# Phase ends with a written TensorE order, and weight splits held behind the first h, in a one-core encoder step

## The chip, the cores and the metric

The kernel runs on one core of a Trainium2 chip. The metric is the device time of one execution in microseconds (us). Engines are named as in the profile: PE is TensorE's matmul, PEld its weight load, DVE VectorE, ACT ScalarE, POOL GpSimd and SP SyncE, whose queue issues nearly all DMAs here.

## The reference: what is computed

One step of a streaming encoder of two layers, width 1024, on 384 tokens: 256 of one prompt sequence and 8 x 16 of eight sample sequences. Each layer has three sub-layers (FFN, mixer, FFN). Each normalises the residual x, modulates it per sequence, and adds its gated result:

```python
def _modulate(x, g, shift, scale):
    return _rmsnorm(x, g) * (1 + scale[:, None, :]) + shift[:, None, :]

sc = jax.nn.silu(c)
for l in range(DEPTH):                       # DEPTH = 2
    mod = (sc @ prm['ada_w'][l] + prm['ada_b'][l]).reshape(c.shape[0], N_MOD, D_MODEL)   # N_MOD = 9
    x = x + 0.5 * mod[:, 2][:, None] * _swiglu(_modulate(x, g[0], mod[:, 0], mod[:, 1]), ...)
    h = _modulate(x, g[1], mod[:, 3], mod[:, 4])
    mix = ...                                # attention: two kinds in layer 0, one in layer 1
    x = x + mod[:, 5][:, None] * mix
    x = x + 0.5 * mod[:, 8][:, None] * _swiglu(_modulate(x, g[2], mod[:, 6], mod[:, 7]), ...)
y = _rmsnorm(x, prm['final_norm_g'])
```

The adaLN product `sc @ ada_w` gives 9 modulations of 1024 columns for each layer and 9 conditioning rows (one prompt, eight samples).

## The kernel before

**Layout.** The residual lies transposed, as eight tiles `xT[d]` of 128 features x 384 tokens. The input of a phase lies as `hT[0][d]` (high part) and `hT[1][d]` (rest) in the same shape: every dense product is made of three matmuls, high x high, high x rest and rest x high, so that float32 operands keep their precision.

**Weights.** `Stream` holds all dense weights as units in the order of their use. `dma()` (L179) loads a unit raw through SP; `split()` makes its two parts, a cast on ACT (L187, `wh`) and a subtraction on DVE (L188, `wl`), into three buffers, and then issues further loads, up to four raw tiles ahead. `next()` first splits until three units are there (`ahead`), so a split stands in the program well before its product; its raw tile is free for the next load once L188 is done. An FFN's first products run in `feature_half` (L501, L502 with the high part of h, then L508 with the rest): a unit is four tiles of h by 256 columns, 24 matmuls, and two units make a group.

**adaLN.** `Ada` makes one modulation at a time, in 11 steps: eight steps of four matmuls (L302), each on its own 32 columns of the array, against one 512 KB weight tile; a copy to SBUF (L307); two transposes (L311); additions on DVE (L315 and after). Each step frees its weight tile and asks for the next load (L284). Four tiles fit in general; during an FFN a pool of its own gives room for four more. `ada.step(n)` puts n steps into the program at that place, `ada.upto` sets how far steps may go.

**Phase ends.** Five times, at the ends of the first FFN, the mixer and the second FFN of layer 0, and of the first FFN and the mixer of layer 1 (ends 1 to 5 below), `close` (L483) adds the last one (FFN) or two (mixer) tiles to the residual, and makes the next phase's norm. Tiles before that have gone through `Norm.full`, which sums their squares into `acc` on POOL (L406, L408); the last ones go through `gate_p` (L474) and `gate_s` (L480, L481) on DVE and `tail` (two squares on ACT, L414; L422). `sums` (L429) sums the squares over the features with one-column matmuls, for each of three token blocks over `acc` and then the late tiles; `rstd_of` makes the root (L376) and the reciprocal (L378); `spread` scales the identity (L437, L439) and multiplies it by ones (L441), so that each token's factor stands on all partitions. `h` then makes the eight tiles: for the prompt L455 (DVE), L457 (ACT), L458 (DVE), for the samples L463 (POOL), L464 (DVE), L466 (ACT), L467 (POOL). At its end `close` puts one whole modulation (`ADA_STEPS`, 11 steps) into the program:

```python
        norm.spread(norm.sums(range(3)))
        norm.h()
        ada.upto(*norm.filled)
        ada.step(ADA_STEPS)
```

**Order.** Nothing here fixes the order on an engine. A planner orders the instructions of each engine ahead of time: it goes by costs of its own, ranks by the place in the program, and puts what is ready into holes. So adaLN steps and splits, which stand behind the norm in the program, run inside its waits where the planner sees room. On the chip each engine then takes its instructions in the planned order.

Of the kernel before, what the change touches and what calls it, by code (L numbers as in the profile page):

```python
# [17 lines left out]
D = 1024  # L18
KD = 8
# [19 lines left out]
class Weave:  # L39
    """Work in stages, advanced in turn between the dense products."""  # L40
# [46 lines left out]
    def over(self, slots):  # L87
        """A callback that spreads what is queued over so many calls."""
        count = iter(range(slots, 0, -1))
        return lambda: self.pace(next(count, 1))  # L90
# [14 lines left out]
def kernel(  # L105
# [43 lines left out]
    # ------------------------------------------------------------ constants  # L149
# [13 lines left out]
    # ------------------------------------------------------------ weights  # L163
    class Stream:
        """Weights in the order of their use: loaded in units, split exactly into two parts of 12 bits each."""

        def __init__(self):
            self.units = []
            self.nd = self.ns = self.nu = 0
            self.depth = 2  # L170
            self.tiles, self.parts = [], {}

# [10 lines left out]
        def split(self):  # L183
# [3 lines left out]
            act.copy(out=h, in_=src)  # L187
            dve.tensor_tensor(out=lo, in0=src, in1=h.bitcast(F32), op=ALU.subtract)  # L188
# [9 lines left out]
        def next(self, held=0):  # L198
            """The next unit; the last held ones are still in use."""
# [40 lines left out]
    def add_out(w, parts):  # L240
        """parts: the pairs of rows that a pass over all columns takes."""
# [26 lines left out]
    # ------------------------------------------------------------ adaLN: one modulation of 1024 columns at a time  # L268
# [3 lines left out]
    class Ada:  # L272
# [15 lines left out]
        def ahead(self):  # L288
            """Loads as far as there is room; what a phase's own pool holds is used within the phase."""
# [31 lines left out]
        def finish(self, l, m, d, n):  # L321
            """A factor of a norm becomes 1 + itself, times the gain; a gate of an FFN is halved."""
# [8 lines left out]
        def half_load(self, pl, m, half):  # L331
            """Half of the columns of a modulation of the first norm."""
# [29 lines left out]
        def upto(self, l, m):  # L362
            """Steps past this modulation are put off."""
# [9 lines left out]
    # ------------------------------------------------------------ norms  # L373
# [7 lines left out]
    def warm(x):  # L381
        """The table of the square root, in time."""
# [8 lines left out]
    class Norm:  # L391
        """The norm of the residual and its modulation: full() as tiles become final, tail() for the last ones."""
# [30 lines left out]

        def sums(self, blocks):
# [7 lines left out]
        def spread(self, rs):  # L432
            """The factors of the tokens, over the partitions."""
# [11 lines left out]
        def h(self, ds=range(KD)):  # L445
            for d in ds:
                new_h(d)
                self.h_prompt(d, self.bc)
                self.h_sample(d, self.bs)

        def h_prompt(self, d, bc):
# [5 lines left out]
            act.activation(out=h, in_=u, func=AF.Identity, bias=sh, scale=1.0)  # L457
            dve.scalar_tensor_tensor(out=lo, in0=u, scalar=sh, in1=h.bitcast(F32), op0=ALU.add, op1=ALU.subtract)  # L458
# [24 lines left out]
    def close(l, mod, ds, ys, norm):  # L483
        """The last tiles of the residual, and the norm; a modulation of a later product fills the wait."""
# [4 lines left out]
        norm.spread(norm.sums(range(3)))  # L489
        norm.h()  # L490
        ada.upto(*norm.filled)
        ada.step(ADA_STEPS)

    # ------------------------------------------------------------ FFN
# [99 lines left out]
    def out_half(l, ks, d0, mod, slot, done=None, left=None):  # L594
        """Four of the tiles, over pairs of rows ks, gated and added to the residual."""
# [33 lines left out]
    def token_chunk(n, weave, slots):  # L629
        """Token-major product over n columns: banks of prompt blocks 0 and 1, and of the sample tokens."""  # L630
# [13 lines left out]
    def token_cols(slot):  # L644
        """Token-major product over 256 columns: a bank for each block of tokens."""
# [22 lines left out]
    def soft_rows(S, regions, scale, P, n_rows=128):  # L668
        """Unnormalised exponentials of the rows of S over each region into P; the reciprocals of their sums."""
# [917 lines left out]
```

## Time and profile before

| | us |
|---|---|
| median of 3 runs | 1668.05 |
| lowest, highest | 1667.81, 1672.78 |
| span of the profiled execution, first to last instruction | 1666.9 |
| TensorE busy in it | 1637.8 |
| VectorE busy, ScalarE busy, GpSimd busy | 781.7, 648.9, 125.5 |

The times do not say which run the profiled one is closest to; beside the span no other time of the profiled execution is given. Its mean granted TensorE clock is 0.996 of full speed. In the rows, a matmul of float32 operands on 32 columns appears as two records, and so does a one-column sum; a timeline merges neighbours of one kind (x20 means 20 records), gives the start, the time from the first one's start to the last one's end, and in brackets the idle time before it with what ended it. Matmuls overlap, so the next one starts before the row's end.

### The profile page before, as it was taken

To read this page: it belongs to the slowest core of one execution; us is meant where nothing else is said; L and a number is where in the kernel's file an instruction comes from. 1 tells how busy PE (TensorE), PEld (TensorE's weight loads), DVE (VectorE), ACT (ScalarE), POOL (GpSimd) and SP (SyncE) were. 2 spreads that over 40 slices of the span, in tenths; PEclk is the share of its full clock that TensorE was granted. 3 is DMA by queue.
4 is the path that set the end of the run, shared out by engine and by line. 5 is a ranking of instruction groups with operands and counts; after the bars stand their busy time and mean duration, and the time that the engine had idled before them with its cause. 6 is when DMAs were issued, how large, how long until landed. Compare 5 with 4: busy or idle time off the path is not lost.

```text
span 1666.9 us, 27050 instructions
## 1 busy us (share of the span) xinstructions
PE 1637.8 (98%) x10877; PEld 1496.5 (90%) x10877; DVE 781.7 (47%) x1500; ACT 648.9 (39%) x1205; POOL 125.5 (8%) x186
## 2 busy tenths in 40 slices
PE   7999999999999999999999999999999999999998
PEld 5999999977777799999989999998888879999998
DVE  4543334444466843344453433436554675343334
ACT  4433322353445533333243333324555554333334
POOL 2000001110000300000120000002000012000021
PEclk9999999999999999999999999999999999999999
DMA  9855555482464765663465555345777664444344
GB/s 333 291 157 161 176 158 167 134 275 67 140 209 135 251 165 147 182 192 116 130 210 175 154 165 170 120 122 164 254 230 238 190 207 138 127 127 127 120 123 143
DMA packets 235136, 287.14 MB, mean 172 GB/s; under 512 B 11834, under 2 KB 205154, under 8 KB 235011
## 3 DMA queue, kind: packets, MB, share of 16 engines
q1 hardware_dynamic: 234754, 285.24, 54.9%
q8 instruction: 86, 1.41, 0.4%
q14 instruction: 40, 0.32, 0.1%
q0 software_dynamic: 112, 0.10, 0.0%
q10 hardware_dynamic: 144, 0.07, 0.0%
HBM read 268.10 MB, written 17.27 MB: 171 GB/s over the span
## 4 chain that ended last, share of the span: by engine, by line
PE 94%; DVE 2%; issue 1%; DMA 1%; ACT 1%; POOL 0%; POOLq 0%; ACTq 0%; DVEq 0%
PE bank L501 16%; PE bank L508 15%; PE bank L502 15%; PE bank L264 12%; PE bank L265 11%; PE bank L266 11%; PE bank L302 4%; PE bank L663 2%; PE bank L1224 1%; PE bank L1292 1%; PE bank L839 0%; DMA ada<-in_ada_w_dram 0%; PE bank L344 0%; PE bank L1273 0%; PE bank L973 0%
## 5 line engine op out<-in xcount | busy, mean ns | idle before, releaser
L188 DVE TENSOR_TENSOR wl<-raw,wh 128x1024 fp32r<-128x1024 f32 (+1 forms) x338 | 402.3, 1192 | 612.5 <-ACT wh L187 611.6
L187 ACT CAST wh<-raw 128x1024 fp32r<-128x1024 f32 (+1 forms) x338 | 345.1, 1022 | 611.2 <-PE bank L508 243.7
L501 PE MATMUL bank<-h,wh 128*128 128x384 f32 x1472 | 499.2, 341 | 3.8 <-ACT h L466 3.8
L502 PE MATMUL bank<-h,wl 128*128 128x384 f32 x1472 | 492.2, 336 | 0.0
L501 PEld LDWEIGHTS bank<-h,wh 128*128 128x128 f32 x1472 | 276.2, 188 | 26.0 <-issue 10.4
L508 PE MATMUL bank<-h,wh 128*128 128x384 f32 x1472 | 287.8, 335 | 0.0
L502 PEld LDWEIGHTS bank<-h,wl 128*128 128x128 f32 x1472 | 276.4, 188 | 3.2 <-issue 1.8
L508 PEld LDWEIGHTS bank<-h,wh 128*128 128x128 f32 x1472 | 257.8, 188 | 0.6 <-issue 0.5
L264 PE MATMUL bank<-ah,wh 128*128 128x384 f32 (+1 forms) x704 | 235.1, 334 | 0.0
L266 PE MATMUL bank<-al,wh 128*128 128x384 f32 (+1 forms) x704 | 233.5, 332 | 0.0
L265 PE MATMUL bank<-ah,wl 128*128 128x384 f32 (+1 forms) x704 | 233.5, 332 | 0.0
L264 PEld LDWEIGHTS bank<-ah,wh 128*128 128x128 f32 x704 | 132.3, 188 | 3.3 <-issue 2.9
L265 PEld LDWEIGHTS bank<-ah,wl 128*128 128x128 f32 x704 | 132.3, 188 | 0.0
L266 PEld LDWEIGHTS bank<-al,wh 128*128 128x128 f32 x704 | 132.3, 188 | 0.0
L264 PE MATMUL bank<-wh,h 128*128 128x256 f32 (+3 forms) x312 | 103.8, 335 | 0.1
L266 PE MATMUL bank<-wl,h 128*128 128x256 f32 (+3 forms) x312 | 98.7, 317 | 0.0
L265 PE MATMUL bank<-wh,h 128*128 128x256 f32 (+3 forms) x312 | 98.4, 316 | 0.2 <-POOL h L467 0.2
L532 ACT ACTIVATE s<-bank 128x384 f32<-128x384 f32 x88 | 38.5, 489 | 130.7 <-PE bank L508 130.7
L302 PE MATMUL bank<-ada,scT 128*32 128x256 f32 x1024 | 83.3, 390 | 2.9 <-DMA ada<-in_ada_w_dram 2.3
L538 DVE TENSOR_TENSOR a<-s,bank 128x384 f32<-128x384 f32 x88 | 44.9, 551 | 78.7 <-PE bank L508 78.7
L264 PEld LDWEIGHTS bank<-wh,h 128*128 128x128 f32 x312 | 59.0, 190 | 12.3 <-issue 9.7
L265 PEld LDWEIGHTS bank<-wh,h 128*128 128x128 f32 x312 | 59.2, 190 | 3.5 <-issue 0.8
(311 smaller groups left out, 1543.7 us busy)
## 6 DMA issues: line engine op xcount, KB each, us to landing
raw<-in_ffn_w_in_dram SPq DMA_DIRECT2D x176, 512.0 KB, 3.8
ada<-in_ada_w_dram SPq DMA_DIRECT2D x128, 512.0 KB, 4.6
raw<-in_ffn_w_out_dram SPq DMA_DIRECT2D x68, 512.0 KB, 3.5
raw<-in_ffn_w_out_dram SPq DMA_DIRECT2D x34, 384.0 KB, 3.1
raw<-in_c_w_in_dram SPq DMA_DIRECT2D x24, 512.0 KB, 4.8
half<-in_ada_w_dram SPq DMA_DIRECT2D x16, 512.0 KB, 10.0
out_dram<-kv SPq DMA_DIRECT2D x32, 224.0 KB, 5.2
raw<-in_ab_w_in_dram SPq DMA_DIRECT2D x12, 512.0 KB, 5.5
```

The costliest lines, as they stand in the source:

```text
L187: act.copy(out=h, in_=src)
L188: dve.tensor_tensor(out=lo, in0=src, in1=h.bitcast(F32), op=ALU.subtract)
L264: pe.matmul(out=out, lhsT=wh, rhs=xh, start=start, stop=False)
L265: pe.matmul(out=out, lhsT=wl, rhs=xh, start=False, stop=False)
L266: pe.matmul(out=out, lhsT=wh, rhs=xl, start=False, stop=stop)
L302: pe.matmul(out=ps[32 * g:32 * g + 32, 0:256], lhsT=scT[:, k, :], rhs=t[:, g * 256:(g + 1) * 256], start=(k == 0), stop=(k == KD - 1), til ...
L501: pe.matmul(out=out, lhsT=w[0][:, kk, ms], rhs=hT[0][k], start=(k == 0), stop=False)
L502: pe.matmul(out=out, lhsT=w[1][:, kk, ms], rhs=hT[0][k], start=False, stop=False)
L508: pe.matmul(out=banks[mi][:, 0:NT], lhsT=w[0][:, kk, mi * 128:(mi + 1) * 128], rhs=hT[1][k], start=False, stop=(k == KD - 1))
L532: act.activation(out=s[mi], in_=g[mi][:, 0:NT], func=AF.Silu)
L538: dve.tensor_tensor(out=a, in0=s[mi], in1=u[mi][:, 0:NT], op=ALU.mult)
L663: pe.transpose(out=ps[0:m, i * 128:(i + 1) * 128], in_=src, identity=ident)
```

## The change

`close` now writes TensorE's order out, in a region in which TensorE issues its instructions in the order of the program: the sums of `acc` for three blocks, three adaLN steps, the sums of the late tiles, three adaLN steps, the spread, two adaLN steps. What else falls in between on TensorE, and the other engines, stay the planner's. The three last steps of the modulation come behind h. All sums of a norm now go into one accumulation (`sum_part`), of which the first matmul alone starts anew. `h` returns its prompt instructions, and the next two splits after a phase end are ordered behind those of tiles 1 and 3: the cast behind that tile's L457 on ACT, the subtraction behind its L458 on DVE, as an order on the engine and not a wait. Nothing else is changed; the diff also drops docstrings and comments, which make no instruction.

```diff
+    def behind(later, first):
+
+        tc.add_manual_dep(later.ins if hasattr(later, "ins") else later, (first.ins if hasattr(first, "ins") else first).name,
+                          mybir.DependencyInfo(mybir.DependencyClass.NoSync, mybir.DependencyReason.DATA), reason="order")
...
             self.tiles, self.parts = [], {}
+            self.after = []
...
-            act.copy(out=h, in_=src)
-            dve.tensor_tensor(out=lo, in0=src, in1=h.bitcast(F32), op=ALU.subtract)
+            cast = act.copy(out=h, in_=src)
+            sub = dve.tensor_tensor(out=lo, in0=src, in1=h.bitcast(F32), op=ALU.subtract)
+            if self.after:
+                for later, first in zip((cast, sub), self.after.pop(0)):
+                    behind(later, first)
...
+        def sum_part(self, ps, sq, blocks, first=False):
+
+            for i, b in enumerate(blocks):
+                pe.matmul(out=ps[:, i:i + 1], lhsT=sq[:, b * 128:(b + 1) * 128], rhs=ones[:, 0:1], start=first and i == 0, stop=True, skip_group_check=True)
...
         def h(self, ds=range(KD)):
+            made = []
             for d in ds:
                 new_h(d)
-                self.h_prompt(d, self.bc)
+                made.append(self.h_prompt(d, self.bc))
                 self.h_sample(d, self.bs)
+            return made
...
-        norm.spread(norm.sums(range(3)))
-        norm.h()
         ada.upto(*norm.filled)
-        ada.step(ADA_STEPS)
+        with tc.manual_schedule(engines={mybir.EngineType.PE}):
+            ps = bank()
+            norm.sum_part(ps, norm.acc, range(3), True)
+            ada.step(3)
+            for sq in norm.late:
+                norm.sum_part(ps, sq, range(3))
+            ada.step(3)
+            norm.spread(rstd_of(ps[:, 0:3], 3, D))
+            ada.step(2)
+        made = norm.h()
+        stream.after = [made[1], made[3]]
+        ada.step(ADA_STEPS - KD)
```

## Rows read from the trace of the kernel before

**Rows 1.** From the page: the span, the first engine of its part 1 (busy us, share of the span, instructions), and the chain that ended last by engine.

```profile
span 1666.9 us, 27050 instructions
PE 1637.8 (98%) x10877; PEld 1496.5 (90%) x10877; DVE 781.7 (47%) x1500; ACT 648.9 (39%) x1205; POOL 125.5 (8%) x186
PE 94%; DVE 2%; issue 1%; DMA 1%; ACT 1%; POOL 0%; POOLq 0%; ACTq 0%; DVEq 0%
```

**Rows 2.** Busy time of each engine in the stretches from a phase's last product to the next phase's first, at ends 3 and 4; then the granted clock and DMA.

```profile
852.27:860.01 7.74, 7.10 (x81) 3.68 (x80) 4.67 (x12) 3.51 (x10) 1.69 (x4) 1.00 0.84 253
1149.84:1159.84 10.00, 8.44 (x99) 4.33 (x98) 7.11 (x16) 4.19 (x10) 2.77 (x6) 1.00 0.87 272
```

**Rows 3.** Timeline of TensorE at end 3, from the first sum to the spread.

```profile
852.11 0.28 PE L429 MATMUL bank<-ones,acc 128*128 128x1 f32 x2
852.32 1.49 PE L302 MATMUL bank<-ada,scT 128*32 128x256 f32 x20
...
853.98 0.36 PE L429 MATMUL bank<-ones,acc 128*128 128x1 f32 x2
...
854.43 0.36 PE L429 MATMUL bank<-ones,acc 128*128 128x1 f32 x2
854.72 0.63 PE L302 MATMUL bank<-ada,scT 128*32 128x256 f32 x6
855.28 0.38 PE L429 MATMUL bank<-ones,sq 128*128 128x1 f32 x2
855.60 1.50 PE L302 MATMUL bank<-ada,scT 128*32 128x256 f32 x24
857.03 0.91 PE L441 MATMUL bank<-dg,ones 128*128 128x384 f32 x2
```

**Rows 4.** The same of end 5: the third adaLN piece, and the spread.

```profile
1374.23 0.62 PE L302 MATMUL bank<-ada,scT 128*32 128x256 f32 x2 [0.28 <-DMA ada<-in_ada_w_dram]
1375.13 0.88 PE L441 MATMUL bank<-dg,ones 128*128 128x384 f32 x2 [0.28 <-DVE dg L439]
```

**Rows 5.** Timeline of VectorE among the gates: end 1, end 4, end 5.

```profile
326.00 0.83 DVE L188 TENSOR_TENSOR wl<-raw,wh 128x640 fp32r<-128x640 f32 x1
...
1152.62 0.23 DVE L481 TENSOR_TENSOR xT<-gt,xT 128x128 f32<-128x128 f32 x1
...
1370.11 1.22 DVE L188 TENSOR_TENSOR wl<-raw,wh 128x1024 fp32r<-128x1024 f32 x1
1371.24 0.29 DVE L481 TENSOR_TENSOR xT<-gt,xT 128x128 f32<-128x128 f32 x1
```

**Rows 6.** VectorE while h is made: two L458 one tile apart, behind end 3 (timeline), and all L464 of the kernel (least, median and greatest ns).

```profile
861.13 0.47 DVE L458 SCALAR_TENSOR_TENSOR h<-up,modT,h 128x256 fp32r<-128x256 f32 x1
...
862.39 0.47 DVE L458 SCALAR_TENSOR_TENSOR h<-up,modT,h 128x256 fp32r<-128x256 f32 x1
...
L464 DVE TENSOR_TENSOR us<-us,modT x48: 273/544/551, 23.2 to 1385.9; 128x128 f32<-128x128 f32 x48
```

**Rows 7.** Timeline of TensorE at end 1 (first sum, spread) and end 4 (spread); windows that cut a merged row show it alone.

```profile
325.04 0.28 PE L429 MATMUL bank<-ones,acc 128*128 128x1 f32 x2
...
330.37 0.59 PE L441 MATMUL bank<-dg,ones 128*128 128x384 f32 x1
...
1156.30 0.59 PE L441 MATMUL bank<-dg,ones 128*128 128x384 f32 x1
```

**Rows 8.** Four adaLN loads ahead of end 5: the first in the chain that ended last (start, us), the four issues on SP's queue (ns, first and last start), and the issue to landing of the last.

```profile
1358.24 3.85 DMA ada<-in_ada_w_dram
...
L284 SPq DMA_DIRECT2D ada<-in_ada_w_dram x4: 341/376/384, 1358.2 to 1359.6; - x4
...
DMA to landing us min/median/max: 6.1/6.1/6.1
```

**Rows 9.** Timelines behind end 2, where the last tiles of h are made: VectorE, GpSimd, ScalarE, TensorE.

```profile
575.72 1.22 DVE L188 TENSOR_TENSOR wl<-raw,wh 128x1024 fp32r<-128x1024 f32 x1
576.85 1.28 DVE L458 SCALAR_TENSOR_TENSOR h<-up,modT,h 128x256 fp32r<-128x256 f32 x2
...
575.95 1.30 POOL L467 TENSOR_TENSOR h<-us,h 128x128 fp32r<-128x128 f32 x1 [0.90 <-ACT h L466]
...
576.19 0.28 ACT L466 CAST h<-us 128x128 fp32r<-128x128 f32 x1
...
577.42 1.55 PE L508 MATMUL bank<-h,wh 128*128 128x384 f32 x8
```

**Rows 10.** Timeline of TensorE in the second FFN: the last adaLN records of the modulation begun at end 2, and the product behind one of the pieces.

```profile
602.82 0.62 PE L302 MATMUL bank<-ada,scT 128*32 128x256 f32 x2
...
628.21 0.63 PE L302 MATMUL bank<-ada,scT 128*32 128x256 f32 x6
628.77 0.45 PE L501 MATMUL bank<-h,wh 128*128 128x384 f32 x1
...
633.51 0.64 PE L302 MATMUL bank<-ada,scT 128*32 128x256 f32 x8
```

**Rows 11.** adaLN matmuls (L302) alone, in five stretches from the last product of a phase to the end of the next phase's first group (at end 1: of its first four units): us, PE busy (records), PEld busy, clock, DMA; the first, the last and the sum of the five, whose records are 90, 48, 66, 82 and 64.

```profile
325.20:346.70 21.50, 6.81 (x90) 2.75 (x90) 1.00 0.91 302
...
1369.47:1388.95 19.48, 5.51 (x64) 1.90 (x64) 1.00 0.49 175
sum 100.97, PE 27.99 PEld 10.80; mean PE 5.60 PEld 2.16
```

More of the change, by code (lines that the diff above doesn't have):

```diff
@@ L456, in h_prompt @@
             h, lo = hT[0][d][:, PR], hT[1][d][:, PR]
-            act.activation(out=h, in_=u, func=AF.Identity, bias=sh, scale=1.0)
-            dve.scalar_tensor_tensor(out=lo, in0=u, scalar=sh, in1=h.bitcast(F32), op0=ALU.add, op1=ALU.subtract)
+            return (act.activation(out=h, in_=u, func=AF.Identity, bias=sh, scale=1.0),
+                    dve.scalar_tensor_tensor(out=lo, in0=u, scalar=sh, in1=h.bitcast(F32), op0=ALU.add, op1=ALU.subtract))
         def h_sample(self, d, bs):
```

## The prediction, made blind

> **What bounds the kernel now.** I read the page first. TensorE is busy for 98% of the span and holds 94% of the chain that ended last [rows 1], so two things can move the time: work that TensorE does, and moments in which it has none. The change touches five places, the ends of the phases, so next I read the stretches from the last product of a phase to the first product of the next. The shortest is end 3 with 7.74 us, the longest end 4 with 10.00, both at granted clock 1.00, the upper of the two levels [rows 2]; no term below comes from the clock. TensorE looks busy there, but mostly with adaLN steps that fill the wait for a chain: gates (DVE), squares (ACT), sums (PE), root (ACT), reciprocal and diagonal (DVE), spread (PE), h (DVE, ACT, POOL).
>
> The timeline of TensorE at end 3 [rows 3] shows the order that the planner chose: one sum, adaLN, sums, adaLN, the last sum, adaLN, spread. The 64 records of a modulation are 8 steps of four matmuls side by side, two records each. A piece of 20 records takes 1.49 us and one of 6 takes 0.63, so a pass of four costs (1.49 - 0.63) / 2 = 0.43 and a piece 0.20 on top; a cut pass costs a whole one: at end 5 a piece of 2 records takes 0.62 [rows 4]. The timeline of VectorE at ends 5 and 1 [rows 5] has a weight split (L188: 1.22 us, or 0.83 for the narrower units at end 1) in the middle of the gates, just ahead of L481, for whose result the square of the sample tokens waits.
>
> After the spread VectorE is full: the three operations on a tile of h come round every 1.26 us (861.13 to 862.39 [rows 6]), and in an FFN a tile's products take TensorE only 4 x 0.17 = 0.70 (8 matmuls take 1.55, the last one's tail included [rows 9]). So for the first 10 us of a phase VectorE sets the pace, not TensorE.
>
> **The change, part by part.**
>
> *Order of sums, adaLN and spread.* Nothing is added: the same sums, 8 steps and spread. At end 3, from [rows 3]: three sums of the accumulator from 852.11 at a pitch of 0.225 (853.98 to 854.43 for two) reach 852.79; three steps start at 852.85 and let TensorE go 1.43 later (855.60 to 857.03), at 854.28; the last of three late sums starts at 854.73 instead of 855.28. Three more steps follow 0.32 behind it and the spread comes at 856.48 instead of 857.03: 0.55 us earlier. The split in the gates matters less than it looks, since the late sums now stand behind three steps anyway. The same 4.37 us behind the first sum puts the spread of end 1 at 329.41 instead of 330.37 [rows 7]: 0.96 earlier. At end 4 L481 starts as late as 1152.62, behind a memset [rows 5]. If that keeps its place, the squares end near 1153.2, the last sum starts at 1153.65 and the spread at 1155.40 instead of 1156.30 [rows 7]: 0.90 earlier, and some 1.3 more if the memset moves away; I keep the smaller gain.
>
> Ends 2 and 5 close the mixers, which hold only four adaLN buffers, so tiles 5 to 8 are loaded while the steps run. End 5 already waits for the DMA of tile 5 at 1374.23, and the spread is let past after one matmul of it [rows 4]. The new order must finish tiles 5 and 6 first. One sum more stands ahead of step 1 (0.225), whose end frees the buffer, so tile 5 lands at about 1374.45. Of four such loads the first, issued at 1358.24, landed after 3.85 us and the last, issued at 1359.6, after 6.1 [rows 8]: 1.23 apart. That puts tile 6 at 1375.7, its pass behind it, and the spread at 1376.1 instead of 1375.13: 1.0 later. Bounds: 0.3 later if tile 6 lands only one pass (0.43) behind tile 5; 0.8 earlier if neither is late, as at end 3; I take the measured spacing. End 2 has the same buffers and sums, and I give it the same 1.0. Over the five chains: -0.96 + 1.0 - 0.55 - 0.90 + 1.0 = -0.41 us.
>
> *Splits behind h.* No split is added, and one that stands in the gap costs little, because VectorE is waiting there. Behind the second and fourth h it stands where VectorE has no free time. At an FFN's end one of the two held splits comes from the gap (the other waits for its buffer until the phase is under way, and stands there today); at a mixer's end both do. That is one of 0.83 at end 1 and 2 + 1 + 1 + 2 of 1.22 at ends 2 to 5: 0.83 + 6 x 1.22 = 8.15 us of VectorE put ahead of later h. Queued behind a held subtraction are the next tiles' L455, L458 and L464, for which ACT, POOL and then the products wait; behind the held cast stands the next h on ACT. Lower bound nothing, if planner and hardware find holes; upper bound 8.15. Today's split inside the stretch at end 2 [rows 9] is nearly free, because its subtraction (575.72) delays only the last two L458, whose products come last; one behind tile 1 or 3 is ahead of everything, so I take 8.15, less what TensorE has in hand: the last h is there at 576.47 and the last part of the second half starts at 577.42, 0.95 later where the tile's products need 0.70. So 0.25 at each of ends 2 to 5: -1.0.
>
> Could POOL catch up during a subtraction, so that the next L464 takes its least, 0.27, instead of its median of 0.54 [rows 6]? That would give back 0.27 for each of seven splits, 1.9 in all. The row says no: a POOL L467 that ran beside the split at 575.72 took 1.30 us, until 577.25, past the split's end at 576.94 [rows 9]. The Trainium skill, page "SBUF — State Buffer", section "Who interferes with whom", says that a VectorE instruction with two SBUF inputs and a GpSimd instruction that reads SBUF exclude each other; by it the sum stays, without it the sum would be 1.9 lower.
>
> A held split also releases its raw buffer later, so the weight load that waits for it moves some 7 us back on SP's queue. It serves a unit several units (of 24 matmuls, 4.2 us each) ahead, and no longer stands ahead of adaLN loads; I cost it at nothing, and at one wait of 1 to 2 us if a unit does come late.
>
> *What goes into the longer waits.* At end 2 the last 16 of the 64 records stand today among the dense products, in pieces of 2, 6 and 8 [rows 10]; from the start of one to the next product is 0.56 us (628.21 to 628.77). In the new order they run before the first product: -1.7. At ends 1, 3 and 4 the planner already pulls later steps into the stretch (end 1 has 90 records of adaLN in it, 26 more than a modulation [rows 11]); as VectorE holds TensorE up for longer, I count one step more at each, 3 x 0.56 = -1.7, with the bounds 0 and -1.7.
>
> **Sum.** -0.41 + 8.15 - 1.0 - 1.7 - 1.7 = +3.3 us. The profiled execution's span of 1666.9 becomes 1670.2; the median of the runs lies 1.15 above that span, so the time is 1668.05 + 3.3 = 1671.4, 0.2% slower: inside the 0.3% (5 us) that I take as the least that a measurement tells from no change.
>
> **Rivals.**
> - *A, slower: the held subtractions fall behind the last h.* The planner ranks h first, and VectorE has no hole. An FFN's first group needs its second unit some 6 us after its first product; a subtraction later than that decides it. At end 2 the last L458 would end at 578.13 - 1.22 + 1.0 = 577.91 and the subtraction at 579.13; 23 matmuls at 0.174 and the last one's tail then end at 583.3 instead of 578.97 [rows 9], +4.3, less the 1.7; at end 5 the same +4.3; end 1 even; ends 3 and 4 keep their 0.55 and 0.90. +5.5: 1673.5. For it: the ranks. Against: today's subtraction at 575.72 got in ahead of two L458.
> - *B, slower: nothing of the stretch is hidden.* Neither the 1.0 nor the second 1.7 come: +6.0, 1674.1. For it: POOL is blocked along with VectorE. Against: the steps pulled in today.
> - *C, faster: only TensorE's own work counts.* If every wait is filled with adaLN that is needed anyway, as 98% busy suggests, what matters is that no pass is cut. From the ends to the end of the first group, adaLN takes 27.99 us for 90 to 64 records in each stretch, 350 in all [rows 11]. Uncut, 350 / 8 passes at 0.43 are 18.8, and three pieces at each end 15 x 0.20 = 3.0: 21.8. -6.2: 1661.9. Against: at end 5 there is no later modulation to fill with, and VectorE sets the pace behind each spread.
> - *No effect* lies within the forecast: at end 3 the fixed order is nearly the old one.
>
> **Chances.** Forecast 0.41, A 0.16, B 0.14, C 0.29. So faster by over 0.3% 0.29, within 0.41, slower 0.30. The range goes from 1661, just under C, to 1676, which is B with a late weight unit (2 us); the forecast's own goes from 1667 (no effect, or holes for half of the splits) to 1673.
>
> **What would show it.** Right: spreads 4.4 us behind the first sum at ends 1 and 3, and about 1 us later than now at ends 2 and 5, with a wait for DMA in the second three steps; L188 close behind the second and fourth L458; a last L458 that stands 1.2 us (2.4 at ends 2 and 5) further from the spread. A shows as TensorE waiting for wl in the first group; C as first groups that end no later than now, with adaLN pieces of 24, 24 and 16 records. The prediction is wrong if spreads don't wait for tile 6, if splits find holes that these rows don't show, or if the planner, set off by the new order, rearranges adaLN among the dense products, at 0.56 us for each piece.

## The result, and the profile after

The changed kernel takes 1685.94 us (median; 1684.51 to 1687.74) against 1667.93 us for the kernel before on the same chip: ratio 1.0102, 95% interval 1.0087 to 1.0116. It is 18 us slower, far outside the forecast range. The page of the kernel after: span, TensorE, and the chain that ended last, by engine.

```profile
span 1684.8 us, 27051 instructions
PE 1643.0 (98%) x10877; PEld 1497.5 (89%) x10877; DVE 781.3 (46%) x1500; ACT 646.8 (38%) x1205; POOL 118.9 (7%) x186
PE 92%; DVE 3%; issue 2%; ACT 1%; DMA 1%; POOL 0%; POOLq 0%; ACTq 0%; DVEq 0%
```

Beside [rows 1] the instructions of TensorE are the same 10877, but they are busy 5.2 us longer, and TensorE stands idle in the other 12.7 us of the 17.9 by which the span grew. The same number of instructions at a longer duration is a first hint of a lower clock, no more.

Where the time went is seen best by phase. Each end begins with TensorE's first sum, so the starts of these sums cut the span into six phases. The table holds the length of each phase in the profiled execution, less the same phase of the kernel before (325.04, 234.19, 292.88, 297.57, 219.63 and 297.58 us); the experiments of the next section are in it too.

```
                 to end 1  end 1-2  end 2-3  end 3-4  end 4-5  from end 5
after              +0.01    -0.15   +11.83    +0.29    +1.10    +4.83
no_hold            +0.60    -1.63   +12.44    -1.00    +0.30    +0.59
hold_only          +0.12    -1.82    +3.37    +0.24    -0.58    +3.73
early_spread       +0.15    -3.18    +8.44    -1.01    +0.33    -0.65
held_ranked        +0.46    -1.88   +12.58    -0.31    +0.23    +2.38
end2_only          +0.40    -1.81   +12.52    -0.01    +1.34    +0.70
mod_first          +0.42    -2.53    +5.85    -1.00    +0.31    -0.30
ffn_order          -0.24    -2.37    +0.51    -1.01    +0.30    +1.31
ffn_then_free      -0.45    +0.24    +1.32    -1.02    +0.35    +1.00
three_ends         +0.57    -4.40    +0.73    -0.98    -0.16    -0.81
four_ends          -0.33    -2.72    -0.02    -1.00    +0.31    -1.03
```

The phases between ends 1 and 2 and between ends 4 and 5 are the mixers. Between ends 1 and 2 the last four runs and mod_first have the same order written and the same adaLN records in the mixer, and range from -4.40 to +0.24; between ends 4 and 5 runs that leave end 4 as it was range from -0.58 to +1.34. So single microseconds of these two columns mean nothing. The phase that begins at end 2 holds two thirds of the loss, the phase that begins at end 5 another quarter.

End 3 went as forecast. TensorE there, to be read beside [rows 3]:

```profile
863.80 0.72 PE L436 MATMUL bank<-ones,acc 128*128 128x1 f32 x6
864.45 1.50 PE L311 MATMUL bank<-ada,scT 128*32 128x256 f32 x24
865.88 0.83 PE L436 MATMUL bank<-ones,sq 128*128 128x1 f32 x6
866.64 1.50 PE L311 MATMUL bank<-ada,scT 128*32 128x256 f32 x24
868.08 0.91 PE L455 MATMUL bank<-dg,ones 128*128 128x384 f32 x2
```

Two uncut pieces of 24 records, no wait, and the spread 4.28 us behind the first sum instead of 4.92. End 2 has the same program and looks otherwise (TensorE again, from the first sum to the first product):

```profile
559.09 0.83 PE L436 MATMUL bank<-ones,acc 128*128 128x1 f32 x6 [0.45 <-POOL acc L417]
559.85 1.50 PE L311 MATMUL bank<-ada,scT 128*32 128x256 f32 x24
561.28 1.50 PE L436 MATMUL bank<-ones,sq 128*128 128x1 f32 x12
562.71 0.64 PE L311 MATMUL bank<-ada,scT 128*32 128x256 f32 x8
564.80 0.64 PE L311 MATMUL bank<-ada,scT 128*32 128x256 f32 x8 [1.46 <-DMA ada<-in_ada_w_dram]
567.54 1.08 PE L311 MATMUL bank<-ada,scT 128*32 128x256 f32 x8 [2.10 <-DMA ada<-in_ada_w_dram]
568.55 1.65 PE L455 MATMUL bank<-dg,ones 128*128 128x384 f32 x2
...
571.98 0.69 PE L526 MATMUL bank<-h,wh 128*128 128x384 f32 x1 [0.76 <-ACT h L482]
```

The second three steps wait 1.46 us for adaLN tile 5 and 2.10 for tile 6, and the spread, which needs neither, comes 9.46 us behind the first sum, where it came 5.92 before. The last 8 records take 1.08 us instead of 0.64, and the spread's two matmuls 1.65 instead of 0.9. The windows behind show why (us, TensorE busy, PEld, DVE, ACT, POOL, then granted clock, DMA share and GB/s):

```profile
562.00:566.00 4.00, 1.99 (x23) 1.01 (x23) 0.66 (x3) 0.66 (x2) 0.00 (x0) 1.00 0.84 287
566.00:570.00 4.00, 2.46 (x10) 0.70 (x10) 0.00 (x0) 0.00 (x0) 0.00 (x0) 0.58 0.99 356
570.00:574.00 4.00, 3.24 (x20) 1.23 (x19) 3.42 (x8) 3.05 (x7) 3.06 (x7) 0.50 0.71 233
574.00:578.00 4.00, 4.00 (x19) 3.73 (x16) 4.00 (x12) 3.30 (x9) 3.10 (x7) 0.64 0.50 154
578.00:582.00 4.00, 4.00 (x34) 2.98 (x33) 4.00 (x10) 3.07 (x8) 1.48 (x3) 1.00 0.09 12
```

Behind the wait TensorE was granted its lower level (0.50 is 1.2 of 2.4 GHz) until about 577, while the first products already ran; the kernel before holds 1.00 throughout this place. The DMA share is 0.99 in the window in which TensorE waits. The change did not add that load: the kernel before has shares of 0.95 and 1.04 in its windows from 562 to 566 and from 566 to 570, at a clock of 1.00. What is new is that the spread now stands behind the whole of tiles 5 and 6.

The rest of that phase's loss lies in the FFN that follows. First the whole stretch from the spread of end 2 to the first sum of end 3, of the kernel before and of the kernel after:

```profile
565.15:852.11 286.96, 285.83 (x1684) 277.88 (x1685) 122.99 (x170) 99.12 (x140) 17.64 (x23) 1.00 0.53 158
```

```profile
568.55:863.80 295.25, 292.84 (x1741) 281.24 (x1737) 125.29 (x175) 100.66 (x143) 15.72 (x23) 0.99 0.55 164
```

It is 8.29 us longer with 57 more TensorE records. The adaLN matmuls alone (same columns as [rows 11]), in the mixer ahead of end 2 and in the FFN behind it, before and after:

```profile
344.00:559.00 215.00, 13.87 (x168) 4.72 (x168) 0.98 0.53 169
565.30:852.00 286.70, 8.05 (x94) 2.93 (x94) 1.00 0.53 158
```

```profile
344.00:559.00 215.00, 8.94 (x110) 2.20 (x110) 0.98 0.48 149
568.70:863.50 294.80, 12.15 (x144) 4.30 (x144) 0.99 0.55 164
```

Before, the planner had done 168 records in the mixer; after, 110. The missing 58 did not make the mixer shorter to speak of (-0.15 in the table), but 50 of them came back in the FFN, where TensorE has hardly any gaps, and cost 4.10 us of busy time. Counted from first sum to first sum, the kernel before has 256 adaLN records between ends 1 and 2 and 128 between ends 2 and 3, the changed kernel 192 and 192: one whole modulation of 64 records has moved.

At end 5 the spread comes 6.88 us behind the first sum instead of 5.82. The larger loss comes behind it, in the first group (TensorE, then VectorE):

```profile
1397.71 0.86 PE L526 MATMUL bank<-h,wh 128*128 128x384 f32 x4
1401.48 0.62 PE L527 MATMUL bank<-h,wl 128*128 128x384 f32 x2 [2.91 <-DVE wl L194]
```

```profile
1398.09 1.31 DVE L474 SCALAR_TENSOR_TENSOR h<-up,modT,h 128x256 fp32r<-128x256 f32 x2
1399.33 0.86 DVE L471 SCALAR_TENSOR_TENSOR up<-bank,modT,xT 128x256 f32<-128x256 f32 x2
1400.22 1.21 DVE L194 TENSOR_TENSOR wl<-raw,wh 128x1024 fp32r<-128x1024 f32 x1
1401.35 0.87 DVE L474 SCALAR_TENSOR_TENSOR h<-up,modT,h 128x256 fp32r<-128x256 f32 x2
1402.25 2.35 DVE L194 TENSOR_TENSOR wl<-raw,wh 128x1024 fp32r<-128x1024 f32 x2
```

The held subtraction (L194) is not right behind the second or fourth tile of h; it stands among the last ones, at 1400.22, and TensorE waits 2.91 us for it. In the window from 1402 to 1406, right behind, the granted clock is 0.61. At end 2 TensorE has no such wait for a subtraction.

### The profile page after: what moved, and what is told of

The parts are those of the page before. It is cut to its first block, busy times and chain, and to the rows that moved or that the text cites. A ratio compares the mean times of both kernels' runs of the same rounds, so it can differ in the third digit from the quotient of the medians.

```text
span 1684.8 us, 27051 instructions
## 1 busy us (share of the span) xinstructions
PE 1643.0 (98%) x10877; PEld 1497.5 (89%) x10877; DVE 781.3 (46%) x1500; ACT 646.8 (38%) x1205; POOL 118.9 (7%) x186
## 4 chain that ended last, share of the span: by engine, by line
PE 92%; DVE 3%; issue 2%; ACT 1%; DMA 1%; POOL 0%; POOLq 0%; ACTq 0%; DVEq 0%
PE bank L526 16%; PE bank L527 15%; PE bank L533 15%; PE bank L273 11%; PE bank L275 11%; PE bank L274 11%; PE bank L311 3%; PE bank L688 2%; PE bank L1249 1%; PE bank L1317 1%; DVE us L480 0%; PE bank L864 0%; PE bank L353 0%; PE bank L998 0%; DVE h L474 0%
## 5 line engine op out<-in xcount | busy, mean ns | idle before, releaser
L194 DVE TENSOR_TENSOR wl<-raw,wh 128x1024 fp32r<-128x1024 f32 (+1 forms) x338 | 402.3, 1192 | 609.1 <-ACT wh L193 608.2
L526 PEld LDWEIGHTS bank<-h,wh 128*128 128x128 f32 x1472 | 277.4, 189 | 29.4 <-issue 10.6
```

The costliest lines, as they stand in the source:

```text
L194: sub = dve.tensor_tensor(out=lo, in0=src, in1=h.bitcast(F32), op=ALU.subtract)
L526: pe.matmul(out=out, lhsT=w[0][:, kk, ms], rhs=hT[0][k], start=(k == 0), stop=False)
```

## The experiments

All are compared with the kernel before on the same chip. Unless a diff says otherwise it stands against the changed kernel.

**Without the holds** (no_hold), to split the loss between the two halves of the change:

```diff
-        stream.after = [made[1], made[3]]
```

> The changed kernel with the splits not held behind h; TensorE's order at the ends stays written out. Theory 1 (held subtractions fall behind the last h, and TensorE waits for them at ends 2 and 5): the 2 to 3 us waits for wl in the first groups go, and most of what ends 2 and 5 lost behind the spread with them; what stays is the late spread of ends 2 and 5 and the adaLN that moved into the dense products. 7 to 10 us over the kernel before. Rival (the written order alone costs the 18 us, through its waits for DMA and the lower clock behind them; splits are nearly free): 15 us or more over the kernel before.

Measured: 1679.47 us against 1668.83, ratio 1.0072 (1.0047 to 1.0097), +10.6 us. That is a little above the 7 to 10 of the first theory and far below the rival. By the medians the holds cost some 7 us of the 18; by the table 4.24 of them lie behind end 5. The phase of end 2 is no shorter without them (+12.44), so its loss is the order's.

**The holds alone** (hold_only; against the kernel before, whose close is kept):

```diff
-        norm.h()
+        made = norm.h()
+        stream.after = [made[1], made[3]]
```

> The splits held behind h, TensorE's order at the ends left to the planner as before. Theory 1: the waits for wl at ends 2 and 5 are there (about 3 us each), spreads are where they were or a little earlier, adaLN lies as before: 5 to 9 us over the kernel before. Rival (the written order does it all): within 2 us of the kernel before.

Measured: 1673.48 against 1668.83, ratio 1.0028 (1.0018 to 1.0037), +4.7, just under the 5 to 9 expected. TensorE's waits in this run, from the list of them (total us, times, longest):

```profile
PE bank L519 <- DVE wl L194: 4.0, 2, 2.0
```

Two waits for a held subtraction, one behind each mixer; the kernel before has none. The loss behind end 5 is +3.73, so the hold does there by itself what it does in the changed kernel. Alone the holds cost 4.7 us, on top of the written order some 7; the intervals are too wide to tell the two apart.

**The spread ahead of the tiles that are late** (early_spread; no holds). At the mixers' ends the late sums are followed by one step, and four come behind the spread:

```diff
-            ada.step(3)
+            ada.step(3 if len(ds) == 1 else 1)
             norm.spread(rstd_of(ps[:, 0:3], 3, D))
-            ada.step(2)
+            ada.step(2 if len(ds) == 1 else 4)
         made = norm.h()
-        stream.after = [made[1], made[3]]
```

> Splits not held; written order, but at the two mixers' ends only one adaLN step (tile 4, which is loaded) stands between the late sums and the spread, and four behind it. Theory 1: the spread of end 2 comes at about 564 and that of end 5 about 1.5 us earlier than in the run with the full order and no hold, TensorE's clock stays at its upper level there, and the time is 3 to 5 us below that run, so 3 to 6 over the kernel before; the rest is adaLN among the dense products of layer 0's second FFN. Rival (the wait for tiles 5 and 6 only moves behind the spread, where the products wait for it): within 1 us of that run.

Measured: 1674.40 against 1668.83, ratio 1.0045 (1.0028 to 1.0061), +5.6, 5 us below no_hold. TensorE at end 2:

```profile
559.82 0.64 PE L311 MATMUL bank<-ada,scT 128*32 128x256 f32 x8
561.06 0.88 PE L455 MATMUL bank<-dg,ones 128*128 128x384 f32 x2 [0.60 <-DVE dg L453]
561.87 0.64 PE L311 MATMUL bank<-ada,scT 128*32 128x256 f32 x8
564.38 0.64 PE L311 MATMUL bank<-ada,scT 128*32 128x256 f32 x8 [1.86 <-DMA ada<-in_ada_w_dram]
```

The spread is 4.86 us behind the first sum, the adaLN tile is waited for behind it (1.86 us), while h is made, and the clock stays at 1.00. Still the phase of end 2 loses 8.44 us: the late spread and the clock are not the whole.

**The holds with a place that is enforced** (held_ranked). The splits are issued in the program between tiles of h, so that nothing lets them fall behind:

```diff
-        made = norm.h()
-        stream.after = [made[1], made[3]]
+        stream.after = [norm.h(range(2))[1]]
+        stream.split()
+        stream.after = [norm.h(range(2, 4))[1]]
+        if len(ds) == 2:
+            stream.split()
+        norm.h(range(4, KD))
```

> The changed kernel, but the held splits stand in the program between the tiles of h, so that the planner ranks them ahead of later h: subtractions stand right behind h of tiles 1 to 3 instead of behind the last one. The prediction's price: each pushes the rest of h back by up to 1.22 us, no wait for wl. Theory 1: waits for wl of 3 us at ends 2 and 5 are exchanged for up to 2.4 us of later h: 0 to 4 us below the changed kernel. Rival (a subtraction finds holes on VectorE once it is ranked): the last L474 stands no further from the spread than in the kernel before, and the time falls by 6 us or more.

Measured: 1683.78 against 1668.83, ratio 1.0094 (1.0076 to 1.0112). VectorE behind end 5, the subtractions now among the tiles:

```profile
1391.77 1.48 DVE L194 TENSOR_TENSOR wl<-raw,wh 128x1024 fp32r<-128x1024 f32 x1
1393.17 0.68 DVE L474 SCALAR_TENSOR_TENSOR h<-up,modT,h 128x256 fp32r<-128x256 f32 x1
...
1394.17 0.28 DVE L480 TENSOR_TENSOR us<-us,modT 128x128 f32<-128x128 f32 x1
...
1396.29 1.21 DVE L194 TENSOR_TENSOR wl<-raw,wh 128x1024 fp32r<-128x1024 f32 x1
```

In no_hold one subtraction, too, stands ahead of the last L474 of end 5 (at 1399.31):

```profile
1398.08 1.32 DVE L194 TENSOR_TENSOR wl<-raw,wh 128x1024 fp32r<-128x1024 f32 x1
```

This is the kernel that I had priced. From the spread to the end of the last L474 it takes 14.49 and 14.48 us at ends 3 and 4, against 13.12 and 13.27 in no_hold: 1.4 and 1.2. At end 5 it is 14.07 - 13.11 = 0.96. At each of these ends held_ranked has two subtractions ahead of the last L474 and no_hold has one, so each of these figures is the price of one more, of 1.22. Behind a subtraction the next L480 can take its least, 0.28 at 1394.17; four of the eight at end 5 do, against one in no_hold. TensorE no longer waits for wl behind end 5, and that phase loses 2.38 instead of 4.83. In all it is 15.0 us above the kernel before, 3 less than the changed kernel, since end 2 keeps its loss (+12.58).

**The order at end 2 alone** (end2_only; the other four ends and the splits as in the kernel before):

```diff
+        if l == 0 and len(ds) == 2:
+            ada.upto(*norm.filled)
+            with tc.manual_schedule(engines={mybir.EngineType.PE}):
...
+        else:
+            norm.spread(norm.sums(range(3)))
...
```

> The kernel before with the written order (3, 3 and 2 adaLN steps, as in the changed kernel) at end 2 alone; no split is held, the other four ends are as before. Theory (end 2 is where the order loses: 3.4 us by the wait for its adaLN tile 6, some 2 us by the clock behind that wait, 4 to 6 us by the modulation that it pins out of the mixer): 8 to 12 us above the kernel before, with a lag that rises by 4 us or more between the spread of end 2 and 592 us and by 4 us or more between 592 and 718 us. Rival (only the late spread counts, and the rest came from the other ends or the holds): 2 to 5 us above.

Measured: 1681.59 against 1667.51, ratio 1.0075 (1.0059 to 1.0091), and +12.52 us in the phase of end 2, as in the changed kernel. Its two parts, up to the spread and from there to end 3:

```profile
557.82:566.66 8.84, 5.91 (x66) 3.35 (x66) 4.31 (x11) 2.78 (x7) 0.00 (x0) 0.88 0.67 229
566.66:863.22 296.56, 294.73 (x1749) 280.42 (x1746) 123.46 (x173) 99.56 (x141) 17.51 (x23) 0.99 0.56 166
```

2.92 us of it are the late spread, 9.60 the FFN behind. In all it is 14.1 us, more than the 8 to 12 that I expected. On the same products of the FFN the lag behind the kernel before rises by 4.2 us from the spread to 592 and by 5.6 from there to 718, both the 4 or more of the theory. So one end out of five makes the larger part of the loss, and the rival (2 to 5 us) is out.

**The modulation asked for ahead of the gates** (mod_first; against early_spread), so that it is not inside the written stretch of end 2:

```diff
+        if l == 0 and len(ds) == 2:
+            ada.upto(*norm.filled)
+            ada.step(ADA_STEPS)
+            ada.upto(1, 1)
+        else:
+            ada.upto(*norm.filled)
         for d, y in zip(ds, ys):
             gate_p(l, mod, d, y)
             gate_s(l, mod, d, y)
             norm.tail(d)
-        ada.upto(*norm.filled)
```

> The run with the early spread and no holds, with one difference: at end 2 the modulation that was due there, the third of the second norm's FFN, is asked for ahead of the gates and outside the fixed stretch, so that the planner may again do it in the idle stretches of the mixer; the fixed stretch at end 2 takes eight steps of the next modulation, as the gap did in the kernel before. Theory (the fixed stretch pins that modulation behind the mixer, and 48 to 64 records more then stand between the dense products of the FFN behind end 2): the 6 us that the early-spread run lost in that FFN go away, and the run is at the kernel before or up to 3 us below it. Rival (the loss in that FFN has another cause, for example the clock or the order of the loads): 4 to 6 us above the kernel before, as the early-spread run.

Measured: 1671.37 against 1667.51, ratio 1.0020 (1.0008 to 1.0033): +3.9, just short of the rival's 4 to 6. But the rows say more than the sum. adaLN alone, in the mixer and in the FFN as above, then that FFN as a whole, then the same whole of early_spread:

```profile
344.00:557.00 213.00, 13.45 (x168) 4.47 (x168) 0.99 0.52 170
562.10:855.50 293.40, 7.65 (x96) 1.89 (x96) 0.99 0.53 155
...
561.99:855.85 293.86, 288.33 (x1687) 278.16 (x1688) 122.18 (x170) 99.02 (x140) 17.63 (x23) 0.99 0.53 155
```

```profile
561.06:857.52 296.46, 292.96 (x1753) 280.35 (x1754) 123.71 (x173) 99.22 (x141) 17.74 (x23) 0.99 0.57 169
```

The records moved as the theory says: 168 in the mixer and 96 in the FFN, where the kernel before has 168 and 94, and TensorE's busy time in the FFN falls by 4.63 us. But the stretch is only 2.60 shorter, since TensorE now idles 293.86 - 288.33 = 5.53 us in it where it idled 3.50. Two places make the idle time; the first one (ScalarE, then TensorE):

```profile
682.19 0.87 ACT L561 ACTIVATE s<-bank 128x384 f32<-128x384 f32 x2 [6.81 <-PE bank L537]
682.95 2.94 ACT L193 CAST wh<-raw 128x1024 fp32r<-128x1024 f32 x3
```

```profile
684.05 0.62 PE L530 MATMUL bank<-h,wh 128*128 128x384 f32 x2 [1.77 <-ACT wh L193]
685.31 0.62 PE L531 MATMUL bank<-h,wl 128*128 128x384 f32 x2 [0.64 <-DVE wl L194]
```

Three casts stand in one lump behind an activation (L561) that needs the group's last product, so TensorE waits for the cast and then for its subtraction, 2.4 us, and the same again 20 us later; in the window from 700 to 710 the granted clock is 0.83. So the pinned modulation is one cause, shown and priced at 4 to 5 us of busy time, of which this run gets 2.60 us of time back. It is not the whole: the FFN of mod_first still takes 6.90 us more than that of the kernel before (293.86 against 286.96), 4.40 of them idle. Late casts are a second cause in this run; the changed kernel and early_spread have one such place each in that FFN, with waits of 0.5 us for the cast and 0.6 for the subtraction, and the kernel before, ffn_order and end2_only have none. What in the planner's inputs puts the casts there was not tried and stays open.

**The order at the FFN ends alone** (ffn_order), and **with the sums alone fixed at the mixers' ends** (ffn_then_free, no adaLN in those stretches); no holds in either:

In ffn_order the ends with one tile (`len(ds) == 1`) keep the written order and the others are closed as before; in ffn_then_free these others have

```diff
+            with tc.manual_schedule(engines={mybir.EngineType.PE}):
+                ps = bank()
+                norm.sum_part(ps, norm.acc, range(3), True)
+                for sq in norm.late:
+                    norm.sum_part(ps, sq, range(3))
+                norm.spread(rstd_of(ps[:, 0:3], 3, D))
+            norm.h()
+            ada.upto(*norm.filled)
+            ada.step(ADA_STEPS)
```

> The written order of sums, adaLN, late sums, adaLN and spread stands at the three ends behind an FFN only (ends 1, 3 and 4); the two ends behind a mixer (2 and 5) are closed as in the kernel before, and no split is held. Theory (the order is a small gain wherever its adaLN tiles have landed and no modulation is moved out of the mixers): the run without holds and with an early spread was 0.66 us ahead across end 1, 0.9 across end 3 and 0.4 behind across end 4, so this run should be 0 to 3 us below the kernel before. Rival (the order costs something at the FFN ends too, by the adaLN that stands one step further ahead or by the extra DMA): 2 us or more above the kernel before.

> The written order at the FFN ends, and at the two mixer ends a fixed order of the sums, the late sums and the spread alone, with no adaLN in it; no split is held. Theory (what hurts at the mixer ends is the adaLN in the fixed stretch, not the order of the sums): the modulation moves back into the mixer, TensorE does not wait for an adaLN tile ahead of the spread, and the run is 0 to 4 us below the kernel before. Rival (sums that are no longer interleaved with adaLN as the planner had them cost as well at these ends): 2 us or more above the run that fixes the FFN ends alone.

Measured: ffn_order 1667.15 against 1667.51, ratio 0.9995 (0.9985 to 1.0004); ffn_then_free 1668.64, ratio 1.0009 (0.9999 to 1.0018). The order at the FFN ends costs nothing, and the rival is out. In all seven runs that write end 3 without holds the phase from there is 0.98 to 1.02 us shorter. At end 4 the spread comes 5.31 us behind the first sum instead of 6.62, and yet the phase from there is 0.30 to 0.35 longer in the six runs that write it without holds: no gain is seen. ffn_then_free shows that a fixed order without adaLN in it does not pin the modulation (the phase of end 2 loses 1.32 instead of 12), but it delays the spread at ends 2 and 5 to 6.78 and 6.74 us; it is 1.5 us above ffn_order, which neither theory had.

**What is left worth having** (three_ends and four_ends): ends 1, 3 and 5 written, end 5 with 3, 1 and 4 steps; four_ends writes end 4 as well. Ends that are not named are closed as before; no holds.

```diff
+        if l == 1 and len(ds) == 2:
...
+                ada.step(1)
+                norm.spread(rstd_of(ps[:, 0:3], 3, D))
+                ada.step(4)
...
+        elif len(ds) == 1 and l == 0:
...
+                ada.step(3)
+                norm.spread(rstd_of(ps[:, 0:3], 3, D))
+                ada.step(2)
...
+        else:
+            norm.spread(norm.sums(range(3)))
...
```

In four_ends the second condition is `len(ds) == 1` alone.

> The written order only where a run showed a gain: ends 1 and 3 with 3, 3 and 2 adaLN steps, end 5 with 3 steps ahead of the late sums, one behind them and four behind the spread; ends 2 and 4 are closed as in the kernel before, and no split is held. Theory (the gains of the single ends add: 0.7 to 1 us at each of ends 1 and 3, 0.8 at end 5, and the 0.4 that end 4 lost is not lost): 2 to 4 us below the kernel before, and 1 to 3 us below the run that fixes the three FFN ends. Rival (these gains are of the size by which the planner's orders of the stretches between differ, and do not add up): within 1.5 us of the kernel before.

> As the run with ends 1, 3 and 5 written, and end 4 written too (3, 3 and 2 steps); end 2 is closed as in the kernel before. Theory (at end 4 the 0.9 us by which the chain is shorter is given back, since the planner had put 32 adaLN records ahead of the spread there and the written order has 24, so that 9 more stand later): 0.3 to 1 us above the run with ends 1, 3 and 5. Rival (the earlier spread of end 4 is worth its 0.9 us): 0.5 to 1 us below that run.

Measured, against 1667.95: three_ends 1665.35, ratio 0.9986 (0.9977 to 0.9995); four_ends 1665.42, ratio 0.9983 (0.9975 to 0.9991). TensorE at end 5 of three_ends:

```profile
1367.15 1.50 PE L436 MATMUL bank<-ones,sq 128*128 128x1 f32 x12
1368.58 0.64 PE L311 MATMUL bank<-ada,scT 128*32 128x256 f32 x8
1369.82 1.11 PE L455 MATMUL bank<-dg,ones 128*128 128x384 f32 x2 [0.60 <-DVE dg L453]
```

The spread waits only for its own diagonal (0.60 us), 4.75 us behind the first sum. Both beat the kernel before by 2.5 us, and with it the changed kernel; the intervals tell that from none, though it is less than 0.3%. The total of three_ends is in the range of the theory. That it is the sum of the single gains is not shown: by the table some 1.0 us comes behind end 3 and 0.8 to 1.0 behind end 5, and a gain at end 1 cannot be seen among the columns that mean little. The two runs do not differ, so whether end 4 is worth writing stays open.

## Why the prediction was wrong

The forecast was 1671.4 us; the time is 1685.94. By its own steps:

- **The chains at ends 1, 3, 4 and 5: right in place.** Forecast -0.96, -0.55, -0.90 and +1.0; the spread's distance from the first sum changed by -1.05, -0.63, -1.31 and +1.06. At end 5 tiles 5 and 6 came 1.25 us apart (1387.45 and 1388.70), against the 1.23 taken from [rows 8]. Behind end 4 the gain went again.
- **The chain at end 2: the term was mis-sized.** "End 2 has the same buffers and sums, and I give it the same 1.0": it became 3.54. Its tiles came 2.74 us apart (564.80 and 567.54). The loads on SP's queue there (ns least, median, greatest; first and last start; and their issue to landing):

```profile
L293 SPq DMA_DIRECT2D ada<-in_ada_w_dram x7: 327/328/1211, 560.5 to 571.3; - x7
...
DMA to landing us min/median/max: 4.3/5.7/6.5
```

  Seven loads of 512 KB were issued within 11 us. Tile 6 was asked for at 560.98 and landed at 567.50; five such loads had been issued by then, against four when tile 6 landed at end 5. The DMA share alone does not explain the difference, for at end 5 it was 1.02 in the window from 1386 to 1390. But the DMA engines moved 416 GB/s there, and 356 in the window at end 2. What made the spacing longer is not shown beyond that. It should have been read at end 2 itself, where a load that the kernel before issues at 563.90 takes 7.9 us to land.
- **"No term below comes from the clock": wrong.** The clock was at 1.00 in both windows of [rows 2], but those belong to ends 3 and 4 and have no long wait in them. The change put two at end 2 and one behind end 5, and the clock fell behind them. It fell at end 2 in all four runs with this order written there: 0.50 in the window from 570 to 574 in the changed kernel, no_hold, held_ranked and end2_only. From the windows of the changed kernel from 566 to 578, 4 x 0.42 + 4 x 0.50 + 4 x 0.36 = 5.1 us of clock are lost at most, the first part of it largely while TensorE waited; behind end 5 the window at 0.61 is 4 x 0.39 = 1.6.
- **The modulation at end 2: wrong, with the sign.** I counted -1.7 because 16 records of "the modulation begun at end 2" stood among dense products [rows 10]. I had not asked which modulation that was. The one due at end 2 had been done in the mixer, in gaps that cost nothing, and the records of [rows 10] belonged to the next. Writing the due one into end 2 took its records out of the mixer: 144 records instead of 94 in the FFN, +4.10 us instead of -1.7.
- **8.15 us for subtractions ahead of h: the place was wrong, and the price too high.** "One behind tile 1 or 3 is ahead of everything" took an order behind tile 1 for a place next to it. The casts did follow their tiles at end 2 (572.44 and 576.25), but the subtraction stood at 579.92. From the spread to the last L474, ends 1, 3 and 4 take 11.68, 12.87 and 12.87 us, against 11.67, 13.12 and 13.27 without holds: no tile of h waited. Where the splits are forced ahead (held_ranked), the last L474 of ends 1 to 5 comes 1.13, 0.65, 1.37, 1.21 and 0.96 us later than in no_hold, 5.3 in all, and the median is 4.3 us above that of no_hold. At ends 2 and 5 the forecast counted two splits of 1.22 each, but only one more than in no_hold stands ahead of the last tile there. That GpSimd gives nothing back did not hold throughout either: behind a subtraction L480 was often at its least.
- **Rival A's mechanism is what happened at end 5**: TensorE waits for wl there (2.91 us), with the 4.3 us I gave that end close to the 4.24 by which the phase is longer than in no_hold. At end 2, for which rival A had the same 4.3, the changed kernel has no such wait. I gave it 0.16, on the strength of one subtraction of the kernel before that got in ahead of two L458 [rows 9].
- **Slack (-1.0) and one step more at ends 1, 3 and 4 (-1.7): not there.** Both needed h to be late by the subtractions, which it was not.

Together, by phase: end 2 has 11.83 us = 3.54 for the spread, 4.10 for adaLN records, 1.28 more idle time in the FFN (295.25 - 292.84 = 2.41 against 286.96 - 285.83 = 1.13), and 2.91 left over. The windows from 570 to 578, at 0.50 and 0.64, lie in that stretch and lose up to 3.4 us of clock; I have not taken it further apart. End 5 has 4.83 = 1.06 for the spread, and 3.77 for the wait of 2.91 and the clock behind it. The other phases make 1.25, and the sum is 17.9. The list of what would make the prediction wrong did name the planner's rearranging of adaLN among dense products, but gave it no chance in the range.

## What to carry to other kernels

When an order is written by hand over a place that a planner had filled, first ask which work stood there and where the rest of it had been done: fixing it here can drag work out of gaps that were free elsewhere. Keep whatever waits for a load behind the step that the critical chain needs, as moving the spread ahead of two late tiles did, since a wait there costs its own length and, as at end 2, may cost the clock behind it. An order "behind X" is no place "next to X": it takes a bound off one side only.

## What the runs showed of the hardware

- The granted clock fell from 1.00 to 0.58 and then 0.50 behind the two waits of 1.46 and 2.10 us at end 2, and was back at 1.00 by the window from 578. Ahead of the drop TensorE was busy 1.99 of 4 us. In early_spread, where TensorE waited 1.86 us for a tile at end 2, the clock stayed at 1.00. Behind the single wait of 2.91 us at end 5 it was 0.61. It also fell where TensorE had hardly waited: in ffn_order, whose end 2 is closed as in the kernel before, it was 0.60 in the window from 562 to 566, with TensorE busy 3.53 of 4 us there and 3.92 in the window ahead. In four_ends, with the same close at end 2, it was 1.00. So what decides it is not settled by these runs.
- Loads of the same 512 KB came 1.25 us apart at end 5 and 2.74 us apart at end 2. The DMA share was 1.02 and 0.99 there, at 416 and 356 GB/s, so a full DMA share does not tell how fast a load lands.
